# Gating of the attention and HGRN branches moved from under the gate pairs to under the branch projections, with the gMLP branch projected first

## The chip, the cores and the metric

One core of one Trainium2 chip runs the whole kernel in one launch. The metric is the device time of that core in microseconds. TensorE (PE) does the matrix products, VectorE (DVE) and ScalarE (ACT) the elementwise work, GpSimd (POOL) some elementwise work and a part of the DMA issues, SyncE (SP) issues most other DMAs.

## The reference

One inference step of a hybrid decoder of two layers, D = 1024, on 1024 prompt tokens and 8 x 8 sample tokens. All arrays are float32. Per layer:

```
shift, scale, gate = split(silu(c) @ w_ada + b_ada, 3)
h = rmsnorm(x) * (1 + scale) + shift
qa,ka,va,ga, ub,vb,gb, qc,fc,ic,gc, ma,mb,mc = split(h @ w_in)
ya = sliding-window attention;  yb = gMLP spatial gating;  yc = HGRN2 recurrence
merged = sigmoid(ma) * ((ya * silu(ga)) @ w_br_a)
       + sigmoid(mb) * ((yb * silu(gb)) @ w_br_b)
       + sigmoid(mc) * ((yc * silu(gc)) @ w_br_c)
x = x + gate * (merged @ w_out)
```

It returns x, and per layer the attention window, the recurrence's state and the normalised v rows of the sample tokens.

## The kernel before

**Tiling.** The 1088 tokens lie along the free axis in three chunks of 384, 384 and 320 columns (`CH`); channels lie on partitions, in tiles of 128. Every float32 product is made of three fp32r products of high and low parts (L377 to L379). A weight piece `wr` is loaded by SP and split into `pc`: ACT casts the high part (L341), DVE subtracts (L342).

**Stages of a layer.** First h and the projections of w_in for the three mixers run on PE, with attention, the recurrence and gMLP in between. They leave in DRAM `yd[0]`, `yd[1]` (the outputs of attention and HGRN2), `yd[2]` (that of gMLP, already multiplied by its gate) and `yd[3]`, `yd[4]` (the gates of the first two). Then comes the **gate stage**: the 24 channel tiles of ma, mb, mc, two at a time. Two pairs are computed plainly; the ten others by `gate_pair`, which saves one product in eight by Strassen-like sums. `gate_prefetch` prepares the next pair: four pieces `wr` are split, then POOL combines them in place (L1341 to L1344), and `split_t` casts the sums to `tw` on ACT (L454) and subtracts on DVE (L455). Inside a pair, DVE adds products from PSUM to the slab `su` (L1382, L1385). The pair's last product on PE is added onto the PSUM bank that L1385 reads, so it waits for L1385; on DVE L1385 stands behind the subtractions for `tw`. The sigmoid gates go to DRAM as `g`.

**What runs beside the gate pairs.** Generators in the list `side` are advanced a step at a time by `pump`, once per group of matmuls. One is `gating`: for both gated branches, each of four channel tiles and each chunk, it loads y and g into the slab `gy` through POOL's DMA queue (L1425, L1426), multiplies them on DVE two steps later (L1429), and stores the product `yg` from POOL's queue (L1430). There are 24 such rounds a layer. In layer 0 the other is `ada_wide`: 16 units of the conditioning product for both layers. Each unit loads weights `wada` through SP, makes sixteen small matmuls (L1449) and then, in `ada_rows`, lets ACT copy the result to `gs` (L272), yields, and transposes it on PE (L276) for a reduction on DVE (L279).

**Projection stage.** Three branches, eight output tiles and three chunks make 72 groups of 12 matmuls. `ev_m` takes each group from PSUM: in the first branch DVE multiplies it by the gate `gq` into `mg` (L1561); in the other two DVE multiplies (L1563) and POOL adds (L1564); in the third, ACT and DVE split the sum for the product with w_out. `load_gate` fetches `gq` through POOL's queue, with four buffers (L1534). `load_y` fetches the next branch's `yg` or y into slabs `yr` through SP (L1466) and splits them to high and low parts on ACT and DVE (L1461, L1462). PSUM gives four banks in rotation for the products `mm`.

**What sets the order.** POOL and SP run their instructions in the order of the program. For PE, DVE and ACT a list scheduler writes the order from the program's dependences and its costs; each engine then runs its list in order and waits where an operand is late.

Of the kernel before, what the change touches and what calls it, by code (L numbers as in the profile page):

```python
# [10 lines left out]
F32 = mybir.dt.float32  # L11
F32R = mybir.dt.float32r
# [3 lines left out]
ALU = mybir.AluOpType  # L16
# [132 lines left out]
def build(tc, i, o, L):  # L149
# [17 lines left out]
    def slab(n="s", dt=F32):  # L167
        return sp.tile([128, 1152], dt, tag="slab", name=uid(n))
# [98 lines left out]
    def ada_rows(l, kts, ps):  # L267

        adaT = ada_t[l]
        n = len(kts)  # L270
        sb = small("gs", 256)
        S.copy(sb[:, 0:n * 128], ps[:, 0:n * 128])  # L272
        yield
        pt = ps[:, 256:512]
        for a in range(n):
            T.transpose(pt[:, a * 128:a * 128 + 128], sb[:, a * 128:a * 128 + 128], ident)  # L276
        for a, kt in enumerate(kts):
            d, b = adaT[:, kt, :], bada[l][:, kt:kt + 1]
            V.tensor_reduce(d, pt[:, a * 128:a * 128 + 128].rearrange("p (c r) -> p r c", c=4)[:, 0:9, :],  # L279
                            AX.X, ALU.add)  # L280
            if 8 <= kt < 16:
                V.tensor_scalar(d, d, b, 1.0, ALU.add, ALU.add)
                V.tensor_scalar_mul(d, d, gnorm[l][:, kt - 8:kt - 7])
            else:
                V.tensor_scalar_add(d, d, b)
# [67 lines left out]
    def prep(parts, eng=V, keep=None):  # L353
        return [piece(p, eng, keep) for p in parts]

    T_UNITS = {1, 2, 3, 8, 11, 13, 14}
    units = []
    for l in range(L):
        for m in range(0, MT_G + 24, 2):
            a, b = i["w_in"][l, m], i["w_in"][l, m + 1]  # L360
            if m // 2 in T_UNITS:
                units.append([t_piece(a, b, k0) for k0 in range(0, 8, 2)])
            else:
                units.append([f_piece(x, k0) for x in (a, b) for k0 in (0, 4)])
        for b in range(3):
            for j in range(0, 8, 2):
                units.append([f_piece(i["w_br"][l, b, j + jj], 0) for jj in range(2)])
        for j in range(0, 4, 2):
            units.append([f_piece(i["w_out"][l, j + jj], k0) for jj in range(2) for k0 in (0, 4)])
# [769 lines left out]
    for l in range(L):  # L1139
# [148 lines left out]

        yg = [dp.tile([4, 128, NTOK], F32, tag=f"yg{l}{b}", name=f"yg{l}{b}") for b in range(2)] + [yd[2]]
        gd = [dp.tile([8, 128, NTOK], F32, tag=f"g{l}{b}", name=f"g{l}{b}") for b in range(3)]
        sbl = []
        HB = H[1]
# [63 lines left out]
        def gate_pair(e, w, last):  # L1358
# [29 lines left out]
            if last:  # L1388
                del blk, s2, s3, s4
                sbl[:] = []  # L1390
                y0.append(y_slabs())
                next(ly)
            x = full(mbank())
            product(x, t1, lambda k: a(1, k))
# [20 lines left out]
                    product(p1, lambda k: col(w, 8, 0, k + 4), lambda k: a(0, k + 4), start=False)  # L1415
                    put_gate(e, 0, p1)

        def gating():

            t = slab("gy")  # L1420
            for b in range(2):
                for kk in range(4):
                    for c, (t0, n) in enumerate(CH):
                        y, g = t[:, 0:n], t[:, 384:384 + n]
                        nc.gpsimd.dma_start(y, yd[b][kk][:, t0:t0 + n])  # L1425
                        nc.gpsimd.dma_start(g, yd[3 + b][kk][:, t0:t0 + n])  # L1426
                        yield
                        yield
                        V.scalar_tensor_tensor(y, y, 0.5, g, ALU.mult, ALU.mult)  # L1429
                        nc.gpsimd.dma_start(yg[b][kk][:, t0:t0 + n], y)  # L1430
                        yield

        def ada_wide(cols):

            t = [slab("wada")[:, 0:1024].rearrange("p (a c n) -> p a c n", a=2, c=4) for _ in range(2)]
# [16 lines left out]
                    load(*cols[x + 1])  # L1452
                yield from ada_rows(l, kts, ps)

        def load_y(b, dst, first=False):

            def half(y, kk, c):
                t0, n = CH[c]
                hi, lo = dst(kk, c)
                x = y[:, t0:t0 + n]  # L1460
                S.copy(hi, x)  # L1461
                V.tensor_sub(lo, x, hi.bitcast(F32))  # L1462

            def load(kk):
                y = slab("yr")
                nc.sync.dma_start(y[:, 0:NTOK], yg[b][kk])  # L1466
                return y
            if first:
                ys = [load(kk) for kk in range(4)]
                yield  # L1470
                for c in range(3):
                    for kk in range(4):
                        half(ys[kk], kk, c)
                return
            for kk in range(4):
                y = load(kk)
                yield
                for c in range(3):
                    half(y, kk, c)
                yield  # L1480

        def y_slabs():
            t = [[slab("y", F32R) for _ in range(2)] for _ in range(4)]
            return lambda k, c: [x[:, CH[c][0]:CH[c][0] + CH[c][1]] for x in t[k]]

        def first_y():
            yield from load_y(0, lambda kk, c: y0[0](kk, c), True)
            yield

        y0 = []  # L1490
        ly = first_y()
        sg_ = sums()
        side.append(sg_)
        for e in range(0, 24, 2):
            w = unit()
            if e > 2:
                gate_pair(e, w, e == 22)
                continue
            first_group = True
            for j in range(2):  # L1500
                for c in (2, 0, 1):
                    def ev_s(c, t0, n, ps):
                        put_gate(e + j, c, ps)
                    f_group(w, j, 8, rhs_h, c, ev_s)
                    if first_group:
                        (gate_prefetch if e else prefetch)()
                        first_group = False
            if e == 2:
                drain(sg_)
                for k in range(4):  # L1510
                    split(HB[:, 0, k, :], HB[:, 1, k, :], sbl[1][k])
                sbl[1] = None
                split_t()
                side.append(gating())
                acols = [(0, list(range(16, 24)))] if l == 0 else []
                if l + 1 < L:
                    acols.append((l + 1, list(range(24))))
                if acols:
                    side.append(ada_wide(acols))
        tw[:] = []  # L1520
        drain(*side)
        prefetch()
        rhs_y = y0[0]


        merged, sgs = [], []
        grp = [(b, j, c) for b in range(3) for j in range(8) for c in range(3)]

        def load_gate():
            if grp:  # L1530
# [6 lines left out]
        for b in range(3):  # L1537
            if b == 0:
                Hy = new_H()
                rhs_n = lambda k, c, Hy=Hy: (Hy[c][:, 0, k, :], Hy[c][:, 1, k, :])  # L1540
                ly = load_y(1, rhs_n)
                side.append(ly)
            elif b == 1:
                rhs_n = y_slabs()
                ly = load_y(2, rhs_n)
                side.append(ly)
            else:
                del Hy
                Hm = new_H()
# [18 lines left out]
            if b < 2:  # L1568
                drain(ly)
                rhs_y = rhs_n  # L1570
        del rhs_y, rhs_n, merged, ly, y0
        drain(*side)
        last = l + 1 == L
        if not last:
# [88 lines left out]
```

## Time and profile before

| what | value |
|---|---|
| three runs, median (least, most) | 2418.38 us (2406.66, 2419.66) |
| profiled execution | 2415.48 us |
| its span in the profile | 2413.6 us |
| PE busy | 2275.5 us, 94% |
| DVE busy | 1271.9 us, 53% |
| ACT busy | 796.7 us, 33% |
| POOL busy | 682.1 us, 28% |
| HBM read, written | 194.04 MB, 74.19 MB |

The span is what the profiler saw between the first and the last instruction; the execution's own time is 1.9 us longer. An engine's busy time counts the stretches in which it works on an instruction. PE's idle time, 138.1 us, is the difference of its busy time and the span. The waits of an engine are its idle times grouped by the instruction that waited and by the event that came last before it. The granted clock is the share of full speed, 2.4 GHz, at which TensorE was allowed to run; 0.50 is 1.2 GHz. The gate pairs of layer 0 lie from 696.65 to 974.78 us, those of layer 1 from 1901.16 to 2133.63 (nine intervals each, counted between the same two products of successive pairs), the projections from 994.32 and from 2153.16.

### The profile page before, as it was taken

Reading aid. Unit: us, or ns where it says so; the run is one execution under the profiler, and the core shown is the slowest. Engines: PE = TensorE matmul, PEld = TensorE weight load, DVE = VectorE, ACT = ScalarE, POOL = GpSimd, SP = SyncE. Lnnn points to the kernel's source line nnn. Section 1 sums busy time; section 2 is a strip of 40 time slices with the busy share of each in tenths; the row PEclk is TensorE's granted clock in tenths of the full one; section 3 lists DMA queues with packets and bytes.
Section 4 is the critical chain, followed back from the end, with each engine's and each line's share of the span. In section 5 each row is a group of like instructions: output and inputs, shape, how many; then the busy total and the mean of one; then the engine's idle time right before and its main releaser. Section 6 shows DMA issues by size and latency. Waiting matters only on the chain.

```text
span 2413.6 us, 43577 instructions
## 1 busy us (share of the span) xinstructions
PE 2275.5 (94%) x17170; PEld 2163.9 (90%) x17170; DVE 1271.9 (53%) x2925; ACT 796.7 (33%) x2032; POOL 682.1 (28%) x835
## 2 busy tenths in 40 slices
PE   6999999999997968998999999999999988899998
PEld 5999899999997868998999988999999988899898
DVE  6558656664453333454573586667644533345431
ACT  4445523342132223312233455233322332342110
POOL 3101013242233333166110010132422443324621
PEclk9999999999998989999999999999999989999999
DMA  7222111122245555654332221121222344456431
GB/s 276 74 81 77 62 36 62 49 82 71 78 138 183 195 186 169 190 181 144 109 98 74 75 77 62 36 64 47 87 70 76 114 150 143 148 183 190 150 130 42
DMA packets 134589, 269.12 MB, mean 111 GB/s; under 512 B 21809, under 2 KB 62001, under 8 KB 134353
## 3 DMA queue, kind: packets, MB, share of 16 engines
q1 hardware_dynamic: 85520, 147.55, 19.3%
q0 software_dynamic: 28128, 92.04, 11.6%
q10 hardware_dynamic: 20736, 26.75, 3.1%
q8 instruction: 135, 2.21, 0.4%
q14 instruction: 70, 0.57, 0.1%
HBM read 194.04 MB, written 74.19 MB: 111 GB/s over the span
## 4 chain that ended last, share of the span: by engine, by line
PE 33%; issue 8%; POOL 8%; DVE 6%; DMA 6%; ACT 1%; POOLq 0%; SPq 0%; ACTq 0%; DVEq 0%
PE mm L377 7%; PE mm L378 7%; PE mm L379 7%; POOL mg L1564 3%; DMA gy<-y 3%; DMA yg<-gy 2%; PE mm L431 2%; PE mm L433 2%; PE mm L432 2%; POOL gq L1534 1%; PE av L912 1%; DMA gq<-g 1%; POOL wr L1343 1%; DVE pc L342 1%; POOL wr L1341 1%
## 5 line engine op out<-in xcount | busy, mean ns | idle before, releaser
L377 PE MATMUL mm<-H,pc 128*128 128x384 f32 (+1 forms) x1872 | 625.6, 334 | 1.8 <-ACT pc L341 1.1
L378 PE MATMUL mm<-H,pc 128*128 128x384 f32 (+1 forms) x1872 | 615.0, 329 | 0.0
L379 PE MATMUL mm<-H,pc 128*128 128x384 f32 (+1 forms) x1872 | 614.8, 328 | 0.0
L377 PEld LDWEIGHTS mm<-H,pc 128*128 128x128 f32 x1872 | 352.5, 188 | 19.8 <-issue 14.2
L342 DVE TENSOR_TENSOR pc<-wr,pc 128x512 fp32r<-128x512 f32 x308 | 223.3, 743 | 254.2 <-ACT pc L341 253.0
L378 PEld LDWEIGHTS mm<-H,pc 128*128 128x128 f32 x1872 | 352.7, 188 | 3.8 <-issue 3.2
L379 PEld LDWEIGHTS mm<-H,pc 128*128 128x128 f32 x1872 | 352.3, 188 | 1.1 <-DVE H L455 0.6
L341 ACT CAST pc<-wr 128x512 fp32r<-128x512 f32 x312 | 189.7, 618 | 220.0 <-PE mm L379 106.1
L431 PE MATMUL mm<-pc,H 128*128 128x256 f32 x896 | 259.1, 289 | 0.2 <-DVE gq L1148 0.2
L433 PE MATMUL mm<-pc,H 128*128 128x256 f32 x896 | 254.3, 284 | 0.0
L432 PE MATMUL mm<-pc,H 128*128 128x256 f32 x896 | 253.6, 283 | 0.0
L433 PEld LDWEIGHTS mm<-pc,H 128*128 128x128 f32 x896 | 171.6, 192 | 3.2 <-issue 3.2
L431 PEld LDWEIGHTS mm<-pc,H 128*128 128x128 f32 x896 | 171.6, 192 | 2.2 <-DVE gq L1148 0.5
L432 PEld LDWEIGHTS mm<-pc,H 128*128 128x128 f32 x896 | 171.8, 192 | 0.0
L1429 DVE SCALAR_TENSOR_TENSOR gy<-gy 128x384 f32<-128x384 f32 (+1 forms) x48 | 28.9, 603 | 213.4 <-DMA gy<-y 213.4
L377 PE MATMUL mm<-y,pc 128*128 128x384 f32 (+1 forms) x384 | 127.7, 333 | 13.9 <-DVE gq L1563 13.9
L379 PE MATMUL mm<-y,pc 128*128 128x384 f32 (+1 forms) x384 | 125.5, 327 | 0.0
L378 PE MATMUL mm<-y,pc 128*128 128x384 f32 (+1 forms) x384 | 125.3, 326 | 0.0
L1564 POOL TENSOR_TENSOR mg<-mg,gq 128x384 f32<-128x384 f32 (+1 forms) x90 | 98.9, 1099 | 70.2 <-DVE gq L1563 68.5
L629 POOL TENSOR_TENSOR hk<-hk,ht 128x512 f32<-128x512 f32 (+1 forms) x48 | 69.7, 1453 | 136.9 <-issue 40.3
L1149 POOL DMA_DIRECT2D y<-gq x48 | 26.3, 549 | 288.2 <-DVE gq L1148 111.2
L1534 POOL DMA_DIRECT2D gq<-g x144 | 78.9, 549 | 86.6 <-DVE mg L1561 51.2
(416 smaller groups left out, 4647.8 us busy)
## 6 DMA issues: line engine op xcount, KB each, us to landing
wr<-in_w_in SPq DMA_DIRECT2D x192, 256.0 KB, 3.3
g<-gq ACTq DMA_DIRECT2D x96, 192.0 KB, 2.4
gq<-g POOLq DMA_DIRECT2D x96, 192.0 KB, 2.7
wada<-in_w_ada SPq DMA_DIRECT2D x64, 256.0 KB, 4.0
wr<-in_w_in SPq DMA_DIRECT2D x112, 128.0 KB, 2.6
gy<-y POOLq DMA_DIRECT2D x64, 192.0 KB, 2.8
wr<-in_w_br SPq DMA_DIRECT2D x48, 256.0 KB, 3.9
yr<-yg SPq DMA_DIRECT2D x16, 544.0 KB, 4.4
```

The costliest lines, as they stand in the source:

```text
L341: S.copy(pc[:, 0, :], flat)
L342: eng.tensor_sub(pc[:, 1, :], flat, pc[:, 0, :].bitcast(F32))
L377: T.matmul(ps, w[0], r[0], start=start, stop=False, skip_group_check=True)
L378: T.matmul(ps, w[1], r[0], start=False, stop=False, skip_group_check=True)
L379: T.matmul(ps, w[0], r[1], start=False, stop=stop, skip_group_check=True)
L431: T.matmul(p3(ps), a, wh[k], start=k == 0, stop=False)
L432: T.matmul(p3(ps), a, wl[k], start=False, stop=False)
L433: T.matmul(p3(ps), b, wh[k], start=False, stop=k == 7)
L629: G.tensor_mul(kv[:, :, 0, :], kv[:, :, 0, :], bc_in(tv[:, :, 1], m))
L1429: V.scalar_tensor_tensor(y, y, 0.5, g, ALU.mult, ALU.mult)
L1534: nc.gpsimd.dma_start(sgs[-1], gd[b][j][:, t0:t0 + n])
L1564: (V if b == 2 and j == 7 else G).tensor_add(mg, mg, sg)
```

## The change

The projections take the branches in the order gMLP, attention, HGRN2. gMLP needs no further gating, so its y is what the last gate pair loads. The generator `gating` and the DRAM tiles `yg` are gone. In their place `gated_y` loads a whole channel tile of y and of g (128 x 1088 each) through SP while the branch in front is projected, waits three steps, multiplies in place on DVE and splits the result as before. `ada_rows` yields once more between the copy and the transposes.

```diff
@@ ada_rows
         S.copy(sb[:, 0:n * 128], ps[:, 0:n * 128])
         yield
+        yield
         pt = ps[:, 256:512]
@@ weights, in the order of use
+    BR_ORDER = (2, 0, 1)
-        for b in range(3):
+        for b in BR_ORDER:
             for j in range(0, 8, 2):
@@ gate stage
-        def gating():
-            t = slab("gy")
-            for b in range(2):
-                for kk in range(4):
-                    for c, (t0, n) in enumerate(CH):
-                        y, g = t[:, 0:n], t[:, 384:384 + n]
-                        nc.gpsimd.dma_start(y, yd[b][kk][:, t0:t0 + n])
-                        nc.gpsimd.dma_start(g, yd[3 + b][kk][:, t0:t0 + n])
-                        yield
-                        yield
-                        V.scalar_tensor_tensor(y, y, 0.5, g, ALU.mult, ALU.mult)
-                        nc.gpsimd.dma_start(yg[b][kk][:, t0:t0 + n], y)
-                        yield
...
-                side.append(gating())
@@ loads of y
-            for kk in range(4):
-                y = load(kk)
-                yield
-                for c in range(3):
-                    half(y, kk, c)
-                yield
+        def load(src):
+            y = slab("yr")
+            nc.sync.dma_start(y[:, 0:NTOK], src)
+            return y
+        def gated_y(b, dst):
+            for kk in range(4):
+                y, g = load(yd[b][kk]), load(yd[3 + b][kk])
+                for _ in range(3):
+                    yield
+                x = y[:, 0:NTOK]
+                V.scalar_tensor_tensor(x, x, 0.5, g[:, 0:NTOK], ALU.mult, ALU.mult)
...
+                for c in range(3):
+                    d = [cols(t, c) for t in dst[kk]] if isinstance(dst, list) else dst(kk, c)
+                    split(d[0], d[1], cols(y, c))
...
                 yield
@@ projections
-        grp = [(b, j, c) for b in range(3) for j in range(8) for c in range(3)]
+        grp = [(b, j, c) for b in BR_ORDER for j in range(8) for c in range(3)]
...
-                ly = load_y(1, rhs_n)
+                ly = gated_y(BR_ORDER[1], rhs_n)
...
-                ly = load_y(2, rhs_n)
+                ly = gated_y(BR_ORDER[2], y2)
```

The order of three engines shows what moves. First POOL, in layer 1, around one gate pair: `wr` are the four weight pieces that L1341 to L1344 combine, `gy` the gating's slab, `y` and `yg` the DRAM tiles. Before:

```order
L1430 DMA yg_19603<-gy_20090 128x320
L1425 DMA gy_20090<-y_12845 128x384
L1426 DMA gy_20090<-y_12848 128x384
L1341 TENSOR_TENSOR wr_20322<-wr_20322,wr_20317 128x512
L1342 TENSOR_TENSOR wr_20317<-wr_20317,wr_20307 128x512
L1343 TENSOR_TENSOR wr_20307<-wr_20307,wr_20322 128x512
L1344 TENSOR_TENSOR wr_20312<-wr_20312,wr_20307 128x512
L1430 DMA yg_19603<-gy_20090 128x384
L1425 DMA gy_20090<-y_12845 128x384
L1426 DMA gy_20090<-y_12848 128x384
L1396 TENSOR_TENSOR su_20291<-su_20291 128x384
```

The store and the two loads ahead of the first combination belong to the gating. POOL at the same pair with the change (the lines are one further on):

```order
L1396 TENSOR_TENSOR su_19999<-su_19999 128x384
L1342 TENSOR_TENSOR wr_20230<-wr_20230,wr_20225 128x512
L1343 TENSOR_TENSOR wr_20225<-wr_20225,wr_20215 128x512
L1344 TENSOR_TENSOR wr_20215<-wr_20215,wr_20230 128x512
L1345 TENSOR_TENSOR wr_20220<-wr_20220,wr_20215 128x512
L1396 TENSOR_TENSOR su_20201<-su_20201 128x384
```

Between two pairs' combinations only the sum L1396 is left on POOL.

Next PE, in layer 0, at the transposes of one ada unit: `ada` is the unit's product, `gs` ACT's copy of it, `c` and `mm` products of the gate pair. Before, the unit's own product stands two rows ahead of these:

```order
L379 MATMUL c_919_8184<-sb_7396,pc_7875 128x384
L377 MATMUL c_919_8184<-sb_7489,pc_7875 128x384
L378 MATMUL c_919_8184<-sb_7489,pc_7875 128x384
L379 MATMUL c_919_8184<-sb_7489,pc_7875 128x384
L377 MATMUL c_919_8184<-sb_7562,pc_7875 128x384
L378 MATMUL c_919_8184<-sb_7562,pc_7875 128x384
L379 MATMUL c_919_8184<-sb_7562,pc_7875 128x384
L377 MATMUL c_919_8184<-sb_7635,pc_7875 128x384
L378 MATMUL c_919_8184<-sb_7635,pc_7875 128x384
L379 MATMUL c_919_8184<-sb_7635,pc_7875 128x384
L276 MATMUL ada_8168<-c_ident,gs_8181 128x128 x2
L377 MATMUL mm_8205<-H_139,tw_7996 128x384
```

Twelve matmuls of the pair lie between product and transposes here; at other units there are 24. PE with the change, at the unit in the same place:

```order
L380 MATMUL c_927_8229<-H_140,pc_7860 128x320
L381 MATMUL c_927_8229<-H_140,pc_7860 128x320
L379 MATMUL c_927_8229<-H_140,pc_7860 128x320
L380 MATMUL c_927_8229<-H_140,pc_7860 128x320
L381 MATMUL c_927_8229<-H_140,pc_7860 128x320
L277 MATMUL ada_8176<-c_ident,gs_8189 128x128 x2
L379 MATMUL mm_8078<-H_138,pc_7860 128x384
```

The transposes have moved on into the next group; 36 matmuls lie between here, 24 at the least elsewhere.

Last DVE, in layer 0, where the second branch's projection begins: `mg` is the merged sum, `gq` a gate, `mm` the product in PSUM, `yr` a loaded slab, `y` its low part. Before:

```order
L1561 TENSOR_TENSOR mg_10734<-gq_10748,mm_10767 128x320
L1462 TENSOR_TENSOR y_10784<-yr_10818,y_10783 128x384 x2
L1462 TENSOR_TENSOR y_10784<-yr_10818,y_10783 128x320
L1563 TENSOR_TENSOR gq_10764<-gq_10764,mm_10791 128x384
L1563 TENSOR_TENSOR gq_10780<-gq_10780,mm_10820 128x384
L1462 TENSOR_TENSOR y_10786<-yr_10860,y_10785 128x384 x2
L1462 TENSOR_TENSOR y_10786<-yr_10860,y_10785 128x320
```

Three splits stand between the last product of the first branch and the first of the second. DVE with the change:

```order
L1547 TENSOR_TENSOR mg_10647<-gq_10661,mm_10680 128x320
L1465 SCALAR_TENSOR_TENSOR yr_10723<-yr_10723,yr_10725 128x1088
L1549 TENSOR_TENSOR gq_10677<-gq_10677,mm_10696 128x384
L457 TENSOR_TENSOR y_10780<-yr_10723,y_10779 128x384
L1549 TENSOR_TENSOR gq_10693<-gq_10693,mm_10727 128x384
L457 TENSOR_TENSOR y_10780<-yr_10723,y_10779 128x384
L457 TENSOR_TENSOR y_10780<-yr_10723,y_10779 128x320
L1549 TENSOR_TENSOR gq_10709<-gq_10709,mm_10744 128x320
L1549 TENSOR_TENSOR gq_10740<-gq_10740,mm_10761 128x384
L1465 SCALAR_TENSOR_TENSOR yr_10804<-yr_10804,yr_10806 128x1088
```

The gating product of 1088 columns (L1465) now stands ahead of the second branch's first gate product, and another follows four products later.

## Rows read from the trace of the kernel before

**Rows 1.** Waits of PE, gate pairs of layer 0: total us, times, longest.

```profile
PE ada L276 <- ACT gs L272: 35.4, 7, 7.5
PE mm L377 <- DVE su L1385: 7.3, 2, 7.1
PE c L377 <- DVE adaT L279: 1.2, 1, 1.2
```

**Rows 2.** Waits of PE, gate pairs of layer 1.

```profile
PE mm L377 <- DVE su L1385: 26.3, 8, 5.0
```

**Rows 3.** Windows: length; busy PE, PEld, DVE, ACT, POOL; clock; DMA share; GB/s.

```profile
696.65:974.78 278.13, 234.29 (x1477) 218.06 (x1477) 97.10 (x216) 82.25 (x164) 93.11 (x115) 0.91 0.57 187
952.69:974.78 22.09, 21.93 (x133) 21.61 (x133) 8.32 (x13) 8.35 (x16) 6.08 (x5) 1.00 0.63 200
1901.16:2133.63 232.47, 206.18 (x1190) 203.62 (x1189) 85.80 (x140) 72.98 (x144) 94.47 (x115) 0.95 0.46 150
1901.16:1922.80 21.64, 21.64 (x134) 21.64 (x134) 7.82 (x14) 8.09 (x16) 9.66 (x12) 1.00 0.44 149
```

**Rows 4.** Timeline, layer 1, one wait: start, us, instruction, [idle before <-releaser].

```profile
1922.48 0.55 POOL L1430 DMA_DIRECT2D yg<-gy  x1 [3.43 <-DVE gy L1429]
...
1924.99 0.54 POOL L1425 DMA_DIRECT2D gy<-y  x1 [1.97 <-DMA yg<-gy]
...
1926.08 1.29 POOL L1341 TENSOR_TENSOR wr<-wr,wr 128x512 f32<-128x512 f32 x1
...
1934.99 0.69 PE L377 MATMUL mm<-H,tw 128*128 128x384 f32 x1 [3.71 <-DVE su L1385]
```

**Rows 5.** Waits of POOL, gate pairs of layer 1.

```profile
POOL yg L1430 <- DVE gy L1429: 72.9, 16, 5.5
```

**Rows 6.** Timeline of the clean pair in layer 0, POOL's first combination.

```profile
952.59 1.29 POOL L1341 TENSOR_TENSOR wr<-wr,wr 128x512 f32<-128x512 f32 x1 [2.24 <-DVE pc L342]
```

**Rows 7.** Timeline of layer 0, one wait of the transposes.

```profile
734.68 1.26 POOL L1341 TENSOR_TENSOR wr<-wr,wr 128x512 f32<-128x512 f32 x1 [5.17 <-DMA wada<-in_w_ada]
...
739.59 0.69 PE L276 MATMUL ada<-c_ident,gs 128*128 128x128 f32 x2 [7.04 <-ACT gs L272]
```

**Rows 8.** Windows of the wait in layer 1 and the time after it.

```profile
1931.28:1934.99 3.71, 0.00 (x1) 0.00 (x0) 3.66 (x6) 1.60 (x4) 1.80 (x4) 0.90 0.47 142
1934.99:1940.00 5.01, 5.01 (x16) 5.01 (x17) 0.00 (x0) 0.52 (x1) 1.16 (x2) 0.50 0.81 252
```

**Rows 9.** Timeline of PE in layer 0, two places with ada work.

```profile
722.61 0.38 PE L276 MATMUL ada<-c_ident,gs 128*128 128x128 f32 x2
722.75 0.42 PE L377 MATMUL mm<-H,pc 128*128 128x384 f32 x1
...
860.47 1.07 PE L1449 MATMUL ada<-wada,cT 128*32 128x256 f32 x16
861.47 0.44 PE L377 MATMUL c<-sb,pc 128*128 128x384 f32 x1
```

**Rows 10.** Tile yr: ns least/median/most, starts, forms; last: DMA to landing.

```profile
L1462 DVE TENSOR_TENSOR y<-yr,y x48: 477/551/1501, 977.6 to 2217.6; 128x384 fp32r<-128x384 f32 x32, 128x320 fp32r<-128x320 f32 x16
...
DMA to landing us min/median/max: 3.3/4.4/7.2
```

**Rows 11.** Tile gy: the gating product, and what DVE waited for before it.

```profile
L1429 DVE SCALAR_TENSOR_TENSOR gy<-gy x48: 491/557/1366, 688.2 to 2109.0; 128x384 f32<-128x384 f32 x32, 128x320 f32<-128x320 f32 x16
...
  DMA gy<-y: 213.4, 43
```

**Rows 12.** Windows: first, second and third branch of layer 0's projection.

```profile
994.32:1041.84 47.52, 47.52 (x291) 47.52 (x289) 21.80 (x43) 11.33 (x24) 13.51 (x26) 1.00 0.55 165
1041.84:1089.36 47.52, 47.52 (x291) 47.52 (x290) 29.50 (x47) 10.42 (x21) 35.31 (x45) 1.00 0.65 205
1089.36:1151.00 61.64, 53.57 (x305) 49.72 (x304) 27.64 (x54) 15.72 (x31) 36.94 (x46) 1.00 0.46 138
```

**Rows 13.** Page, costliest groups: POOL's addition.

```profile
L1564 POOL TENSOR_TENSOR mg<-mg,gq 128x384 f32<-128x384 f32 (+1 forms) x90 | 98.9, 1099 | 70.2 <-DVE gq L1563 68.5
```

More of the change, by code (lines that the diff above doesn't have):

```diff
@@ L1280, in build @@
         del VB, UB
-        yg = [dp.tile([4, 128, NTOK], F32, tag=f"yg{l}{b}", name=f"yg{l}{b}") for b in range(2)] + [yd[2]]
         gd = [dp.tile([8, 128, NTOK], F32, tag=f"g{l}{b}", name=f"g{l}{b}") for b in range(3)]
@@ L1453, in ada_wide @@
                 yield from ada_rows(l, kts, ps)
[L1455 to L1469, printed above, removed]
-                yield
-                for c in range(3):
-                    for kk in range(4):
-                        half(ys[kk], kk, c)
-                return
-            for kk in range(4):
-                y = load(kk)
-                yield
-                for c in range(3):
-                    half(y, kk, c)
-                yield
@@ L1482, in y_slabs, with first_y @@
[L1482 to L1488, printed above, removed]
+        cols = lambda t, c: t[:, CH[c][0]:CH[c][0] + CH[c][1]]
+        def load(src):
+            y = slab("yr")
+            nc.sync.dma_start(y[:, 0:NTOK], src)
+            return y
+        def first_y(dst):
+            ys = [load(yd[BR_ORDER[0]][kk]) for kk in range(4)]
+            yield
+            dst += [[slab("y", F32R) for _ in range(2)] for _ in range(4)]
+            for c in range(3):
+                for kk in range(4):
+                    split(*[cols(t, c) for t in dst[kk] + ys[kk:kk + 1]])
+            yield
@@ new lines, in gated_y @@
+        def gated_y(b, dst):
+            for kk in range(4):
+                y, g = load(yd[b][kk]), load(yd[3 + b][kk])
+                for _ in range(3):
+                    yield
+                x = y[:, 0:NTOK]
+                V.scalar_tensor_tensor(x, x, 0.5, g[:, 0:NTOK], ALU.mult, ALU.mult)
+                del g, x
+                if isinstance(dst, list):
+                    dst.append([slab("y", F32R), slab("y", F32R)])
+                for c in range(3):
+                    d = [cols(t, c) for t in dst[kk]] if isinstance(dst, list) else dst(kk, c)
+                    split(d[0], d[1], cols(y, c))
+                del y, d
+                yield
@@ L1490, in build @@
         y0 = []
-        ly = first_y()
+        ly = first_y(y0)
         sg_ = sums()
@@ L1522, in build @@
         prefetch()
-        rhs_y = y0[0]
+        rhs_y = lambda k, c: [cols(t, c) for t in y0[k]]
         merged, sgs = [], []
-        grp = [(b, j, c) for b in range(3) for j in range(8) for c in range(3)]
+        grp = [(b, j, c) for b in BR_ORDER for j in range(8) for c in range(3)]
         def load_gate():
@@ L1540, in build @@
                 rhs_n = lambda k, c, Hy=Hy: (Hy[c][:, 0, k, :], Hy[c][:, 1, k, :])
-                ly = load_y(1, rhs_n)
+                ly = gated_y(BR_ORDER[1], rhs_n)
                 side.append(ly)
             elif b == 1:
-                rhs_n = y_slabs()
-                ly = load_y(2, rhs_n)
+                del y0
+                y2 = []
+                rhs_n = lambda k, c: [cols(t, c) for t in y2[k]]
+                ly = gated_y(BR_ORDER[2], y2)
                 side.append(ly)
@@ L1570, in build @@
                 rhs_y = rhs_n
-        del rhs_y, rhs_n, merged, ly, y0
+        del rhs_y, rhs_n, merged, ly, y2
         drain(*side)
```

1 line of the change is left out of this document (removed).

## The prediction

> **What bounds the kernel now.** I read the summary first: TensorE (PE) is busy for 2275.5 of 2413.6 us, so only its idle 138.1 us and its slow stretches are to be had. The waits of PE come next, cut to the gate pairs, the stretch from which the change takes the gating. Nine pair intervals of layer 0 hold 35.4 + 7.3 + 1.2 = 43.9 us of waits [rows 1], nine of layer 1 hold 26.3 [rows 2]; nearly all stand before two instructions, the transposes of ada and the product that must wait for L1385. The windows show what a pair costs without waiting: 22.09 us with the gating done, 21.64 with it under way but not in the road; the two stretches take 278.13 and 232.47 us, at granted clocks of 0.91 and 0.95 in place of 1.00 [rows 3].
>
> Next, one wait of layer 1, followed back. PE waits 3.71 us for L1385. Ahead of that on VectorE (DVE) stand casts of tw, which need POOL's four combinations L1341 to L1344. L1341 starts only at 1926.08, because in POOL's program order a store of yg and two loads of gy stand in front of it, and these wait for DVE and for the slab's last transfer [rows 4]. POOL spends 72.9 us of this stretch waiting for DVE's gating product before a store [rows 5]. In the clean pair L1341 starts at 952.59, released by the last split of pc [rows 6], and PE then lacks 22.09 - 21.93 = 0.16 us [rows 3]. In layer 0 the same chain ends elsewhere: L1341 comes at 734.68, ScalarE (ACT) casts tw late, the copy gs stands behind that cast, and the transposes wait 7.04 us [rows 7].
>
> A wait costs more than its length. After 3.71 us of idleness the clock falls to 0.50, that is 1.2 in place of 2.4 GHz, for 5.01 us [rows 8]: 2.5 us of work lost besides. Summed: 278.13 against nine clean pairs and the ada work (below) is 61.1 us, of which 43.9 is idle; 232.47 against 198.8 is 33.7, of which 26.3 is idle.
>
> **The change part by part.**
>
> 1. *Gating leaves the gate pairs.* In each layer 24 loads of y, 24 of g, 24 stores and 24 products go. No DMA issue is left between POOL's combinations, so L1341 starts when the splits of pc are done, as in the clean pair. I price a pair at 22.09 us (the slower of the two clean ones, since that one has no gating at all and the other's POOL work was merely in time): layer 1 becomes 9 x 22.09 = 198.8 us, a gain of 33.7.
>
> 2. *One more yield in ada_rows.* The transposes come at least 24 matmuls after the product that feeds them, where 12 were enough before at the places that wait. ada itself stays: 16 units, each sixteen products in 1.00 us and two transposes in 0.14 us, read as the distance to the next start [rows 9], so 16 x 1.14 = 18.2 us. Layer 0 becomes 198.8 + 18.2 = 217.0 us, a gain of 61.1. Parts 1 and 2 can't be told apart here: with POOL in time the copy gs is in time too, and the yield is a second cover. Each alone might do most of it. Bounds for both layers together: at 21.64 a pair, 18 x 0.45 = 8.1 us more gain; at the other end, half of layer 0's loss stays (first rival).
>
> 3. *gMLP comes first.* It has no gate, so its four slabs load as the four gated ones did, in the last pair; its gate loads g stand behind the same slab reuse as before. The weights' order moves with it, the count doesn't. Cost 0, hidden by the last pair's matmuls; if that cover went, one transfer of 4.4 us a layer.
>
> 4. *Gating inside the projection.* Per branch four times: two loads of 544 KB on SP's queue, three yields (three groups of 47.52 / 24 = 1.98 us, so 5.9 us of notice), one product of 128 x 1088 on DVE, then the splits that were there before. Such a slab landed in 4.4 us median, 7.2 at most [rows 10]. The product isn't in the trace at this width. The narrower gating products took 491 ns at the least (320 columns) and 557 at the median (384), so 66 / 64 = 1.03 ns a column and 557 + 704 x 1.03 = 1.28 us; by the worst of them, 1366 ns in place of 557, it would be 3.1 us [rows 11]. Sixteen such products are 20.5 to 50 us more work for DVE; half of them stand in the second branch, beside POOL's additions.
>    - Under the first branch DVE is busy 21.80 of 47.52 us, and POOL 13.51 [rows 12]: 4 x 1.28 = 5.1 us fits. Cost 0. If a product stands ahead of a late operand, what queues behind it are the merge products that free PSUM; four banks rotate, so PE stops only after 3 x 1.98 = 5.9 us.
>    - Under the second branch DVE has 29.50 and POOL 35.31 of 47.52. PE doesn't wait there, but the third branch takes 61.64 us, bound by the chain of DVE, ACT and POOL [rows 12]; lateness that enters it is paid one to one. The first product there (kk = 0) stands ahead of the first gate product on DVE, and its operand g reuses a slab that the last matmul of the first branch reads, so it lands about 4.4 us after that and DVE starts late. Bounds: below 0 I see no reason to go, since nothing leaves that stretch; above, the whole of a load and product for the first, 4.4 + 1.28, and nothing recovered: 5.7 us a layer, about 12 in all with a little for the rest. I take 2 us a layer: 18 us of DVE's 47.52 are free to make it up before the third branch begins, so most of the lateness should be gone by then. So +4, range 0 to 12.
>    - POOL's additions beside DVE's reads: a split of y beside them rose from 551 ns to at most 1501 [rows 10], so operations that meet do lengthen each other, and POOL's addition takes 1.10 us [rows 13]. I hold this to be inside the range 0 to 12. The Trainium skill (SBUF — State Buffer, "two separate sides") says that a DVE operation with two SBUF inputs and a GpSimd operation that reads SBUF lock a shared port pair, the later one blocked for the other's whole instruction. By that rule each of the eight products beside additions would cost one addition, 8 x 1.10 = 8.8 us in place of 4, and the sum would be 2330. That row's 1501 ns, near 551 + 1.10 us, agrees with it; whether it reaches PE no row shows.
>
> 5. *Removed traffic.* The stores of yg and its reading back go; y and g are read as before, only later. In the gate pairs the 150 to 187 GB/s fall by that share. Worth 0: the clean pair has 200 GB/s and doesn't wait [rows 3].
>
> **Sum**, against the profiled execution's own 2415.48 us (span 2413.6 and 1.9 around it): -61.1 - 33.7 + 4 = -90.8, so 2324.7, which I give as 2325. That execution lies 2.9 us under the median of the three, 2418.38, inside their 13 us.
>
> **The rivals.**
>
> - *The chain stays late in layer 0* (0.15). Without gy on POOL, wr's loads still share SP's queue with ada's wide loads: L1341 at 734.68 is put down to the transfer of wada [rows 7], and the new order puts several wr loads behind such a load. For it: that releaser. Against it: in program order POOL had just come from gy's issues, and DVE's last split of pc stood behind the gating product. If half of layer 0's 61.1 us stays, the time is 2325 + 30.5 = 2355.
> - *Waits go, the clock doesn't come back* (0.05). Then only idle time is won: 2415.48 - 43.9 - 26.3 + 4 = 2349. Against it stands the clean pair at 1.00 [rows 3].
> - *The wait moves with the gating: slower* (0.05). DVE waited 213.4 us in 43 places for y and g, 4.96 each [rows 11], and each new product holds the merge products behind it on DVE. If a pair of loads lands later than its notice and PSUM's slack together (twice 5.9 us after issue), nothing covers it, and each of the 16 products costs 4.96 + 3.1 = 8.06 us: 129 us against 94.8 won, so 2415 + 34 = 2450. For it: the notice of 5.9 us is only 1.5 more than the median landing, and both loads share one queue with weights. Against it: the largest landing was 7.2 us [rows 10], and even that is within 11.9.
> - That the change doesn't do what it says: the products are one per four-chunk slab and the gating generator is gone from the order of every engine, so I give this nothing.
>
> **How the numbers follow.** Forecast 0.74, the rivals 0.15, 0.05 and 0.05, the last 0.01 open. The forecast's own range: 2313 (21.64 a pair, no cost in the projection) to 2333 (cost 12). Below, the scatter of the runs, 13 us, takes it to 2305; above, the first rivals take it to 2355, with the slower case (0.05) and the upper part of the first (some 0.07) left out. A difference under 0.5%, 12 us, couldn't be told from none: slower needs the third rival, 0.05; within 0.5% needs some mixture of it with the gain, 0.03; faster is the rest, 0.92.
>
> **What would show it.** Right: both gate stretches near 22 us a pair (24 with ada), granted clock 1.00, no wait over 1 us for L1385's successor or for the transposes; L1341 released by pc's split; first and second branch still 47.5 us, the third up by 2 or so. Part 4 is wrong if PE waits for a merge product in the second branch, or the third grows by over 6 us; part 2 if the transposes still wait in layer 0; part 1 if POOL's combinations start late with no DMA issue ahead of them. A time over 2360 would make the whole argument wrong, for then the gating was not what made the pairs late.

## The result, and the profile after

The changed kernel takes 2333.27 us (median of 4 runs, 2330.83 to 2336.13); the kernel before, run beside it, 2419.02 (2406.66 to 2420.89). The ratio is 0.9656, 95% interval 0.9622 to 0.9691: 85.8 us faster. The forecast was 2325 us, range 2305 to 2355. The profiled execution of run e3 below was a slow one (2722.43 us at a granted clock of 0.755), so e3's time is the median of its other four and its branches are read in e11, the same kernel.

In the gate stage, lines of the changed kernel stand one to two further on for the same code (L1386 is the L1385 of before); in the projections they stand 14 to 16 back (L1549 is L1563, L1550 is L1564). The profiled execution took 2331.80 us, its span is 2330.0; the span before was 2413.6. The summary of the page of after, engines first, then PE's granted clock in 40 slices:

```profile
PE 2257.2 (97%) x17170; PEld 2142.1 (92%) x17170; DVE 1273.0 (55%) x2893; ACT 799.4 (34%) x2032; POOL 611.5 (26%) x691
...
PEclk9999999999999999999999999999999999999999
```

PE is idle for 72.8 us of its span, where it was idle for 138.1. The windows of after: the nine pair intervals of layer 0 and of layer 1, then the first branch, the second and the third of layer 0, and the last two of layer 1 (columns as in [rows 3]):

```profile
697.40:920.28 222.88, 218.68 (x1477) 203.78 (x1477) 87.04 (x192) 81.74 (x164) 57.57 (x45) 1.00 0.52 172
1850.81:2049.12 198.31, 197.08 (x1189) 194.53 (x1189) 74.90 (x117) 75.28 (x144) 55.60 (x45) 1.00 0.34 110
939.81:987.33 47.52, 47.52 (x290) 47.52 (x289) 26.46 (x47) 9.89 (x21) 13.88 (x26) 1.00 0.65 208
987.33:1038.22 50.89, 48.92 (x291) 47.29 (x289) 35.26 (x50) 11.41 (x23) 35.12 (x42) 1.00 0.67 224
1038.22:1098.69 60.47, 51.85 (x291) 46.95 (x289) 26.78 (x54) 15.30 (x30) 37.39 (x48) 1.00 0.48 143
2116.18:2166.85 50.67, 48.62 (x291) 47.32 (x289) 35.36 (x50) 11.41 (x23) 35.36 (x42) 1.00 0.68 225
2166.85:2227.27 60.42, 51.58 (x290) 46.97 (x289) 27.35 (x54) 16.35 (x32) 37.32 (x48) 1.00 0.48 147
```

[Rows 12] end the third branch after some matmuls of the next stage. From its first matmul to the first of w_out it took, before:

```profile
1089.36:1148.36 59.00, 50.93 (x291) 47.08 (x289) 26.25 (x52) 15.26 (x30) 35.25 (x45) 1.00 0.46 138
2248.20:2306.63 58.43, 50.85 (x290) 47.00 (x289) 27.61 (x53) 16.30 (x32) 34.83 (x45) 1.00 0.46 143
```

So the 83.6 us of the spans come apart like this:

| stretch | before | after | difference | forecast |
|---|---|---|---|---|
| nine pairs, layer 0 | 278.13 | 222.88 | -55.2 | -61.1 |
| nine pairs, layer 1 | 232.47 | 198.31 | -34.2 | -33.7 |
| second and third branch, layer 0 | 106.52 | 111.36 | +4.8 | +2 |
| second and third branch, layer 1 | 105.95 | 111.09 | +5.1 | +2 |
| from the last matmul's start to the end | 11.79 | 7.57 | -4.2 | 0 |

What is left comes to under 0.1 us in sum. PE's waits in the pairs, of layer 0 and of layer 1, which answer to [rows 1, 2]:

```profile
PE ada L277 <- ACT gs L272: 4.1, 4, 1.7
...
PE mm L379 <- DVE su L1386: 1.2, 8, 0.2
```

43.9 us have become 4.1, and 26.3 have become 1.2. POOL's waits in layer 1's pairs, which answer to [rows 5]:

```profile
POOL wr L1342 <- DVE pc L343: 106.2, 9, 11.9
POOL su L1396 <- ACT su L1395: 33.9, 9, 3.8
```

All nine first combinations are now released by pc's split; POOL waits long there, and PE hardly waits for what follows from it.

### The profile page after: what moved, and what is told of

It reads as the page before. It is cut to its first block, busy times and chain, and to the rows that moved or that the text cites. A ratio compares the mean times of both kernels' runs of the same rounds, so it can differ in the third digit from the quotient of the medians.

```text
span 2330.0 us, 43307 instructions
## 1 busy us (share of the span) xinstructions
PE 2257.2 (97%) x17170; PEld 2142.1 (92%) x17170; DVE 1273.0 (55%) x2893; ACT 799.4 (34%) x2032; POOL 611.5 (26%) x691
## 3 DMA queue, kind: packets, MB, share of 16 engines
q0 software_dynamic: 19680, 65.29, 8.4%
## 4 chain that ended last, share of the span: by engine, by line
PE 65%; DVE 11%; issue 9%; POOL 8%; DMA 3%; ACT 2%; SPq 1%; POOLq 0%; DVEq 0%; ACTq 0%
PE mm L379 13%; PE mm L380 13%; PE mm L381 12%; PE mm L433 4%; POOL mg L1550 4%; PE mm L435 4%; PE mm L434 4%; PE c L379 2%; PE c L381 2%; PE c L380 2%; POOL gq L1518 1%; PE av L914 1%; DVE pc L343 1%; DMA wr<-in_w_in 1%; PE sc L877 1%
## 5 line engine op out<-in xcount | busy, mean ns | idle before, releaser
L1550 POOL TENSOR_TENSOR mg<-mg,gq 128x384 f32<-128x384 f32 (+1 forms) x90 | 103.4, 1149 | 77.1 <-DVE gq L1549 74.9
L457 DVE TENSOR_TENSOR tw<-wr,tw 128x512 fp32r<-128x512 f32 x80 | 65.6, 850 | 94.4 <-ACT tw L456 94.3
```

Of the source, the lines that this page charges most:

```text
L457: V.tensor_sub(dst_l, src, dst_h.bitcast(F32))
L1550: (V if b == 2 and j == 7 else G).tensor_add(mg, mg, sg)
```

## The experiments

Each ratio is against the kernel before on the same chip. E3, e10 and e11 leave out the multiplication by the gates of attention and HGRN2.

**e1: the second yield alone.** The edit to the kernel before:

```diff
         S.copy(sb[:, 0:n * 128], ps[:, 0:n * 128])
         yield
+        yield
```

> The kernel before with the second yield in ada_rows and nothing else. Theory (POOL's program order is the cause, the yield a second cover): in layer 0 the transposes stop waiting, but the late combinations then hold the pair's last product through L1386, as they do in layer 1. Layer 0's nine pairs fall from 278 to about 250 us, layer 1's stay at 232, the time is about 2390. Rival (the yield does most of layer 0 by itself): layer 0's pairs fall to about 223, as in the changed kernel, and the time is about 2363. If the yield does nothing: 2418.

Measured: 2420.48 us, ratio 1.002 (1.0003 to 1.0037). Layer 0's pairs, and PE's waits in them:

```profile
696.18:983.08 286.90, 233.22 (x1478) 215.56 (x1477) 94.48 (x210) 79.89 (x162) 93.20 (x115) 0.92 0.54 181
```

```profile
PE mm L378 <- DVE su L1386: 32.3, 7, 9.5
PE ada L277 <- ACT gs L272: 20.8, 6, 9.4
```

The theory's 2390 and the rival's 2363 both missed; the third case, that the yield does nothing, has the time right. The transposes' waits fall from 35.4 to 20.8 us, but 32.3 us now stand before the pair's last product, 25 more than before. What is late in a pair still holds PE; the yield only changes at which product.

**e2: the changed kernel without that yield.**

```diff
         yield
-        yield
```

> The changed kernel without the second yield in ada_rows. Theory: with POOL in time, the copy gs is in time too; layer 0's nine pairs take 223 to 233 us, PE's waits for gs stay under 12 us, the time is 2333 to 2343. Rival (the yield does most of layer 0): the transposes wait some 35 us again and the clock falls with them, layer 0's pairs take 260 or more, the time is 2370 or more.

Measured: 2351.27 us, ratio 0.9736 (0.9714 to 0.9758), 18 us above the changed kernel: between the two expectations. Layer 0's pairs, and PE's waits there:

```profile
697.78:940.77 242.99, 226.41 (x1477) 211.07 (x1477) 87.90 (x193) 82.36 (x164) 55.84 (x45) 0.96 0.48 159
```

```profile
PE ada L276 <- ACT gs L272: 16.4, 5, 5.4
```

So the two parts do not add. With the gating in place the yield is worth nothing; with it gone it is worth 18 us (20.1 in layer 0's pairs, 242.99 to 222.88), so something else is still late in layer 0 (see e8).

**e4: gating stays under the pairs, but POOL waits for nothing.** The kernel of e1, with three slabs in turn, loads a round ahead and the store a step later:

```diff
-            t = slab("gy")
+            ts = [slab("gy") for _ in range(3)]
...
+                if x + 1 < len(rounds):
+                    fetch(x + 1)
+                yield
...
                 V.scalar_tensor_tensor(...)
+                yield
                 nc.gpsimd.dma_start(yg[b][kk][:, t0:t0 + n], ...)
```

> The kernel before with the second yield, gating still under the gate pairs and still on POOL's queue, but with three slabs in turn: the loads of a round are issued a round ahead, and its store one step after the product, so POOL waits for neither. Theory (what hurt were POOL's waits ahead of its combinations, not the gating's work): nine pairs take about 225 us in layer 0 and 200 in layer 1, POOL's waits for DVE and for yg nearly vanish, the projections stay as before (47.5, 47.5, 59), the time is about 2325. Rival (DVE's in-order waits for gy, or gating beside the pairs at all, cost it): pairs of 25 us and more in layer 1, time 2380 or more.

Measured: 2334.94 us, ratio 0.967 (0.9646 to 0.9695). The pairs of both layers, then the second branch of layer 0:

```profile
695.71:931.79 236.08, 222.99 (x1478) 207.78 (x1478) 98.70 (x211) 80.70 (x161) 92.32 (x113) 0.97 0.67 221
1856.48:2053.59 197.11, 195.41 (x1189) 194.67 (x1189) 84.35 (x141) 73.85 (x144) 91.95 (x113) 1.00 0.54 175
998.84:1046.36 47.52, 47.52 (x291) 47.52 (x289) 29.88 (x47) 10.31 (x21) 35.31 (x45) 1.00 0.64 204
```

POOL's and DVE's waits for the gating in layer 1's pairs:

```profile
POOL gy L1427 <- DMA yg<-gy: 3.3, 6, 1.4
POOL yg L1437 <- DVE gy L1435: 2.3, 1, 2.3
```

```profile
DVE gy L1435 <- DMA gy<-y: 51.8, 22, 3.9
```

This tells the gating's waits from its work. The same 24 rounds a layer run beside the pairs, 144 DMAs go through the same queue, and layer 1's pairs take 197.1 us, even less than without any gating. POOL's wait for the product fell from 72.9 us to 2.3 [rows 5].

It does not tell a wait on POOL from one on DVE, for DVE's waits for y and g fell too, to 51.8 us from these in layer 1's pairs before:

```profile
DVE gy L1429 <- DMA gy<-y: 96.4, 23, 5.9
```

In the trace of before, this wait stands on DVE ahead of the last splits of pc, for which the first combination, L1341, has to wait as well. In layer 1, at the wait of [rows 4]:

```profile
1921.69 0.49 DVE L1429 SCALAR_TENSOR_TENSOR gy<-gy 128x320 f32<-128x320 f32 x1 [2.00 <-DMA gy<-y]
1922.10 1.89 DVE L342 TENSOR_TENSOR pc<-wr,pc 128x512 fp32r<-128x512 f32 x3
```

The splits end at 1923.99, and L1341 starts at 1926.08. In seven of layer 1's nine pairs it starts 1.6 to 2.1 us after the last split, and that part is POOL's order. In layer 0 it starts 0.14 us after the split in six of nine pairs, so that POOL's order isn't what holds it there; in three of the six the gating product ahead of the split had waited 4.0 to 5.3 us, as here, ahead of the L1341 at 734.68 [rows 7]:

```profile
731.71 0.56 DVE L1429 SCALAR_TENSOR_TENSOR gy<-gy 128x384 f32<-128x384 f32 x1 [3.96 <-DMA gy<-y]
...
733.85 0.68 DVE L342 TENSOR_TENSOR pc<-wr,pc 128x512 fp32r<-128x512 f32 x1
```

Layer 0 of e4 kept 236.1, above the 225 expected. Its longest wait of PE, 8.0 us before the pair's last product, stands behind such a product on DVE:

```profile
787.29 0.49 DVE L1435 SCALAR_TENSOR_TENSOR gy<-gy 128x320 f32<-128x320 f32 x1 [8.92 <-DMA gy<-y]
787.70 0.55 DVE L1386 TENSOR_TENSOR su<-su,mm 128x384 f32<-128x384 f32 x1
```

So the rival's mechanism is there too: it costs little in e4's layer 1, where the longest wait for y and g is 3.9 us, and 8 us at this place in layer 0. In time e4 and the changed kernel can't be told apart (ratios 0.967 and 0.9656, with intervals that overlap).

**e8 and e7: wada's loads on ACT's queue.** In `ada_wide`, of the changed kernel (e8) and of e4's (e7):

```diff
-                        nc.sync.dma_start(t[e][:, a], i["w_ada"]...)
+                        nc.scalar.dma_start(t[e][:, a], i["w_ada"]...)
```

> The changed kernel with the loads of wada issued by ACT instead of SP. Theory (the 4.2 us of waits left in layer 0 come from wr behind wada on SP): they vanish, layer 0's nine pairs take 217 to 219 us, the time is 5 us less, 2328. Rival (ACT's own order sets when gs comes): the waits stay at 4 us or rise, 2333 or more.

> The kernel e4_gating_deep with the loads of wada issued by ACT instead of SP. Theory (what is left in layer 0, the waits of 8.0 and 2.7 us, comes from weight pieces wr standing behind wada's loads on SP): layer 0's nine pairs fall from 236 to about 220 us, the time from 2335 to about 2319. Rival (gating's slab order or POOL's own queue holds layer 0): the waits stay, 2330 or more. If ACT's casts are held by the four more issues a unit, waits of the transposes for gs rise.

Measured: e8 2327.81 us, ratio 0.9646 (0.963 to 0.9663); e7 2346.55, ratio 0.9723 (0.9706 to 0.9741). Layer 0's pairs in e8, where PE has no wait left:

```profile
696.46:914.02 217.56, 217.56 (x1478) 203.98 (x1478) 83.91 (x184) 78.59 (x157) 55.48 (x45) 1.00 0.53 173
```

PE's waits in layer 0's pairs of e7:

```profile
PE mm L378 <- DVE su L1386: 10.8, 4, 4.1
PE ada L277 <- ACT gs L272: 6.0, 3, 2.6
```

In the changed kernel the loads of wada on SP, which hold the wr loads behind them, were the last 5.3 us of layer 0 (222.88 to 217.56; the ratios of the whole times overlap). How SP is held in the changed kernel, in layer 0's pairs, by a wada load that waits for its buffer:

```profile
SPq L1425 <- PE ada L1434: 123.8, 15, 12.1
```

In e4's kernel the same edit cost 12 us (layer 0's pairs took 244.0 in place of 236.1), and its expectation fell. The transposes' waits hardly rose, from 5.1 to 6.0 us. Three of the four waits before the pair's last product stand right behind a gating product that had waited 4.6 to 7.7 us for y and g on DVE, and these waits rose in layer 0 from 43.1 to 81.3 us in all. Why y and g came later no run shows; it stays open.

**e3, e11, e10: what the product under the projections costs.** E3 and e11 are one kernel, without g's loads and without the product; e10 keeps the loads.

```diff
-                y, g = load(yd[b][kk]), load(yd[3 + b][kk])
+                y = load(yd[b][kk])
...
-                V.scalar_tensor_tensor(x, x, 0.5, g[:, 0:NTOK], ALU.mult, ALU.mult)
```

> The changed kernel with the gating left out: gated_y loads y alone and neither loads g nor multiplies, so attention and HGRN2 go ungated into their projections. It prices the gating under the projections. Theory (the products and the loads of g make the second branch late): the second branches fall from 50.9 and 50.7 to 47.5 us, the third from 60.5 to about 59, the time is 10 us less, 2323. Rival (the new order of loads and slabs makes them late, not the products): the branches stay within 1 us of the changed kernel's, the time is 2331 to 2335.

> The kernel of e3 again, with neither g's loads nor the products, for the lengths of its branches: 47.5 us in the second, 59 in the third, and about 2323 us in all, by the theory there; 50 and 60 by the rival.

> The changed kernel that loads y and g under the projections as before but leaves the gating product out (attention and HGRN2 go ungated into their projections). Theory (DVE's products of 1.29 us are what makes the second branch late, not the traffic): the time is that of e3, 2323, and the second branches are near 47.5 us. Rival (the extra loads of g on SP's queue slow the loads of gq and of weights): 2330 to 2334, second branches of 50 us.

Measured: e3 2322.64 us, ratio 0.9612 (0.9586 to 0.9639); e11 2319.85, 0.9604 (0.9583 to 0.9625); e10 2323.09, 0.9614 (0.9595 to 0.9634). Second and third branches of e11, then of e10:

```profile
988.81:1036.33 47.52, 47.52 (x291) 47.52 (x289) 31.13 (x47) 10.42 (x21) 35.62 (x45) 1.00 0.66 208
1036.33:1094.37 58.04, 50.93 (x291) 47.09 (x289) 26.99 (x52) 15.27 (x30) 34.46 (x45) 1.00 0.45 138
```

```profile
990.57:1038.09 47.52, 47.52 (x291) 47.52 (x289) 30.47 (x47) 10.87 (x21) 36.60 (x45) 1.00 0.74 251
1038.09:1096.17 58.08, 50.97 (x290) 47.06 (x289) 27.04 (x52) 15.26 (x30) 34.57 (x45) 1.00 0.46 140
```

Without the product the lateness is gone, with g's loads (251 GB/s) or without them (208). The product is the cause, the traffic is not.

**e5 and e6: why it isn't made up.** E5 loads three gates ahead in place of two; e6 puts the third branch's additions on DVE. Both edit the changed kernel:

```diff
-        for _ in range(2):
+        for _ in range(3):
             load_gate()
```

```diff
-                    (V if b == 2 and j == 7 else G).tensor_add(mg, mg, sg)
+                    (V if b == 2 else G).tensor_add(mg, mg, sg)
```

> The changed kernel with three gate loads ahead instead of two (load_gate called three times before the branches; the same four buffers). Theory (the second branch stays late because a gate's load is issued on POOL only after the addition three groups ahead: 0.55 issue + 2.9 landing + 0.55 product + 1.15 addition = 5.15 us per three groups, 1.72 us against PE's 1.98, so little is recovered): with a fourth group in that loop it is 1.29 us; DVE's waits for gq fall from 12 us to under 4 in the second branch, the second branches from 50.8 to 47.5 to 48.5 us, and the time falls by 4 to 8 us, to about 2327. Rival (the products' own time on DVE, 4 x 1.29 us plus what POOL's additions lengthen, is the lateness): the branches stay within 1 us, the time is 2331 to 2335.

> The changed kernel with the additions of the third branch on DVE instead of POOL. Theory (the third branch runs at 2.5 us a group because of the chain from DVE's product over POOL's addition and ACT's cast back to DVE's subtraction): DVE then does 0.55 + 0.55 + 0.55 us a group, under PE's 1.98, the third branches fall from 60.4 to 50 to 53 us, the time is about 2316. Rival (DVE is then the bound, waiting for ACT's cast in every group): 2.4 us a group or more, the time 2328 to 2340.

Measured: e5 2329.98 us, ratio 0.9663 (0.9645 to 0.9681); e6 2308.86, ratio 0.9568 (0.9551 to 0.9585). Second and third branches of e5, both layers, then of e6:

```profile
986.95:1034.71 47.76, 47.75 (x290) 47.52 (x289) 36.27 (x50) 11.39 (x23) 34.12 (x42) 1.00 0.73 245
1034.71:1096.53 61.82, 52.42 (x290) 46.95 (x289) 26.76 (x53) 15.26 (x30) 38.94 (x49) 1.00 0.46 138
2112.45:2160.07 47.62, 47.62 (x291) 47.51 (x290) 36.34 (x50) 11.49 (x23) 32.69 (x40) 1.00 0.72 242
2160.07:2224.12 64.05, 52.70 (x290) 46.92 (x289) 27.57 (x54) 16.29 (x32) 40.85 (x51) 1.00 0.47 140
```

```profile
989.96:1040.13 50.17, 48.68 (x290) 47.38 (x289) 35.50 (x50) 11.38 (x23) 34.78 (x42) 1.00 0.68 226
1040.13:1088.64 48.51, 47.96 (x290) 47.49 (x289) 36.59 (x73) 15.38 (x30) 16.12 (x28) 1.00 0.59 181
```

E5's second branches are back at 47.6 to 47.8 us, as its theory had it, though DVE's waits for gq fell only from 12.4 to 6.6 us in layer 0's and not to under 4; so the loop through POOL held the lateness there. But the third branches grew to 61.8 and 64.1: what the second gains, the third loses, 1.8 us less in all in layer 0 and 0.6 more in layer 1. The ratio of the whole is no better than the changed kernel's, so the 4 to 8 us expected did not come. E6 shows that POOL's addition is the bound of the third: on DVE the branch takes 48.5 us in place of 60.5, below even the 50 to 53 expected.

**e9: the three edits together**, e8's, e6's and e5's.

> The changed kernel with three edits together: wada loaded by ACT (e8), the third branch's additions on DVE (e6), three gate loads ahead (e5). Theory (each takes away a wait of its own, and with the third branch off POOL the second branch's recovered 2.7 us a layer is no longer handed on): layer 0's pairs take 217.6 us, the second branches 47.7, the third 48.5, and the time is 2309 - 5.3 - 5.4 = 2298. Rival (what e5 recovers in the second branch is lost again in the third, as it was with POOL's additions): third branches of 50 us and more, the time 2303 or more.

Measured: 2294.81 us, ratio 0.9496 (0.9473 to 0.9518), under the 2298 expected. Layer 0's pairs, second and third branch:

```profile
695.89:913.47 217.58, 217.58 (x1478) 204.08 (x1478) 84.41 (x185) 79.20 (x158) 55.47 (x45) 1.00 0.52 173
980.52:1028.40 47.88, 47.73 (x290) 47.49 (x289) 37.32 (x50) 11.39 (x23) 33.88 (x42) 1.00 0.73 243
1028.40:1075.92 47.52, 47.52 (x290) 47.52 (x289) 37.66 (x74) 15.65 (x31) 16.28 (x28) 1.00 0.58 180
```

With POOL out of the third branch, what e5 gains in the second is kept.

**e12: the last drain.** E9's kernel, with one more edit:

```diff
-                nc.gpsimd.dma_start(x_new[j][:, t0:t0 + n], x)
+                nc.scalar.dma_start(x_new[j][:, t0:t0 + n], x)
```

> The kernel of e9 with the stores of x after w_out (48 in all) issued by ACT instead of POOL. It is about POOL's last instruction, a drain, which takes 9.5 us in the kernels with the gating's 144 DMAs on POOL's queue and 5.3 in those without, with nothing else left to run. Theory (the drain grows with the number of DMAs that POOL issued in the run: 4.24 us for 144, 29 ns each): with 48 fewer it takes 5.3 - 1.4 = 3.9 us, and the time is about 1.5 us under e9's. Rival (it belongs to the yg tiles or to the gating alone): it stays at 5.3 us. If a store that waits on ACT holds a cast that PE needs in layer 0's w_out stage, the time rises by a few us.

Measured: 2291.31 us, ratio 0.9487 (0.9461 to 0.9513), the lowest of all, but its interval overlaps e9's, so the gain in time isn't shown. From the last matmul's start to the end it takes 4.1 us, e9 7.6. POOL's drains at the end of the kernel before, of the changed kernel and of e12 (least, median and longest in ns, then the starts of the first and the last):

```profile
L1653 POOLq DRAIN  x3: 40/102/9541, 2403.3 to 2413.4; - x3
```

```profile
L1639 POOLq DRAIN  x3: 40/102/5297, 2323.9 to 2329.7; - x3
```

```profile
L1639 POOLq DRAIN  x3: 40/102/3777, 2192.3 to 2293.6; - x3
```

The long drain is the first of the three in each. It shrinks to 3.78 us, near the 3.9 expected, though e12 has no yg tiles to lose; and it now begins at 2192.3, well before the end.

## Why the prediction was right, and where it was not

1. *Gating leaves the gate pairs: right in size, and in part in mechanism.* Layer 1 came to 198.3 us against 198.8, every pair but the first at 22.09 or within 0.02 of it. That the gating's waits made the pairs late, and not its work, is shown by e4. That it was POOL's program order alone is not: DVE's wait for y and g, in order ahead of pc's splits, held the pairs too, in layer 0 in as many of them as POOL's order did (three each of the nine). In the pairs, the prediction has this wait only as an argument against its first rival. The change takes both away, so its gain doesn't tell them apart. That pairs may take 21.64 with gating beside them, as e4's do, shows that 22.09 was no floor.

2. *The second yield: wrong about one half.* "Each alone might do most of it" fails for the yield: alone it gives nothing (e1), since what is late finds another product to hold. One of the seven waits for gs before, 6.7 us at 852.4, stood behind 24 matmuls already, and not 12. Removing the gating alone gives 65 us (e2, 2416.51 on its chip to 2351.27); the yield on top of it is worth 18 to 20 more. By the sign put on record for this part it was not quite enough: the transposes still wait 4.1 us in layer 0, 1.7 at the longest.

3. *The first rival, wr behind wada on SP:* its mechanism was there, its size was not. I priced it at 30.5 us and gave it 0.15; in the changed kernel it costs 5.3 (222.88 against e8's 217.56), nearly the whole miss of 5.9 in layer 0. The forecast of 217.0 is what the pairs take when that queue is clear. The releaser that spoke for it, wada's transfer at 734.68, is not what released L1341 there: DVE's last split ended 0.14 us before (see e4). Without the yield layer 0 loses 20.1 us more (e2). There, in all five waits, ACT's first cast for the pair had waited 2.3 to 5.5 us for wr, and in four of them SP had issued these wr behind four loads of wada. That fits the same queue, but no edit tried it.

4. *gMLP first and less traffic: right at nothing.* The first branch takes 47.52 us as before, and e10's loads leave the branches as long as e11's.

5. *Gating under the projections: the step that failed.* The product's own price was right: 1.28 us forecast, 1.289 the median of the sixteen. The taken 2 us a layer was too low: it measured 4.8 and 5.1, near the upper bound of 5.7. The third branches grew by 1.5 and 2.0, as forecast; what the sum lacked is the second's growth, 3.4 and 3.1. PE waits there for a merge product, which was the sign that this part is wrong. In layer 0's second branch, and the same in layer 1's:

```profile
PE mm L379 <- DVE gq L1549: 2.0, 4, 0.9
```

   The failing sentence is that DVE's 18 free us would make up the lateness before the third branch. DVE's free time was not what mattered. A gate's load stands on POOL behind the addition of an earlier group, so a late product makes a late addition, a late load and again a late product; e5 breaks that loop and the second branch recovers.

   By the Trainium skill's rule (SBUF — State Buffer, "two separate sides") the sum had 8.8 us for eight products beside additions; the branches of both layers together grew by 9.98. One meeting, in layer 0's second branch of the changed kernel:

```profile
999.43 1.28 DVE L1465 SCALAR_TENSOR_TENSOR yr<-yr,yr 128x1088 f32<-128x1088 f32 x1
999.60 1.99 POOL L1550 TENSOR_TENSOR mg<-mg,gq 128x384 f32<-128x384 f32 x1 [2.36 <-DVE gq L1549]
...
1002.12 1.03 POOL L1550 TENSOR_TENSOR mg<-mg,gq 128x384 f32<-128x384 f32 x1
```

   The addition starts second and takes 1.99 us where the next of its width takes 1.03. The 0.96 us more are most of the 1.11 that it shares with the product (999.60 to 1000.71): the later one is blocked, as the rule has it. Summed over both layers, POOL's 90 additions took 98.9 us before [rows 13], 99.0 in e11, and after:

```profile
L1550 POOL TENSOR_TENSOR mg<-mg,gq 128x384 f32<-128x384 f32 (+1 forms) x90 | 103.4, 1149 | 77.1 <-DVE gq L1549 74.9
```

   So the products lengthened the additions by some 4.5 us, half of the 8.8. That the 9.98 us are made of such meetings isn't shown, since e10 takes the product's own time and the meetings away together. Nor is the 1501 ns of [rows 10] a clean case: that split started 0.37 us ahead of the addition that it met, and it was the split that grew.

6. *The clock came back with the waits*, 1.00 in both layers, so the second rival fell. The third, slower, fell with e11: the products cost some 10 to 13 us and not 129.

7. *Not foreseen:* 4.2 us at the very end, from POOL's drain. Without it the sum, 2324.7, would have missed the profiled 2331.80 by 11 us instead of 7. To that extent the total came as near as it did by luck.

## What to carry to other kernels

An engine that runs its instructions in order should hold none that waits, for a transfer or for another engine, ahead of work that the busiest engine needs: deepen the buffers, or move the waiter. Here the two came to the same time (e4 and the change). When a wait has two causes in line, test each alone and both together, because the one that is removed first may be worth nothing or everything. Free time of an engine does not make up lateness where a ring of buffers ties its next operand to its last result; look at the length of that ring against the pace of the bound.

## What the runs showed of the hardware

POOL's long drain took 9.54 us in all four profiled kernels that issue 446 DMAs on POOL's queue, 5.29 to 5.30 in all nine with 302, and 3.78 in e12's with 254. That is 29 ns a DMA between the first two and 32 between the last two. The packets on that queue fall in step (28128, 19680 and 16864), so the runs can't tell whether it is the DMAs or their packets that count. In the kernel before, the drain ends 7.5 us after the queue's last transfer has landed (2405.39), in the changed kernel 3.2 us after it (2326.01). Both end with a store from POOL, and there the drain lies on the path.
